# Order of the first layer's input: chunk 0's norm and one value block ahead of chunk 1

## The chip, the cores and the metric

The kernel runs on one core of one Trainium2 chip. The metric is the device time of one execution in microseconds (us). Shown is the median of several runs; a profiled execution of its own gives the trace. TensorE (PE), VectorE (DVE), ScalarE (ACT) and GpSimd (POOL) each work through a queue of their own in order; all DMAs are issued from SyncE's queue (SP).

## The reference

A trunk of two layers over 1040 tokens (16 learned ones ahead of 1024), width 1024, everything in float32. Each layer normalizes its input, projects it with one wide matrix, runs two kinds of attention (a differential one and one with a forget gate), gates the result and projects it back:

```python
h = jnp.concatenate([meta, x], axis=1)
for l in range(DEPTH):                       # DEPTH = 2
    hn = rmsnorm(h, norm_gain[l])            # h * rsqrt(mean(h*h) + eps) * gain
    proj = hn @ w_in[l]                      # queries, keys, values, gates
    ...                                      # two attentions, gated: do, fo
    h = h + jnp.concatenate([do, fo], axis=-1) @ w_out[l]
out = rmsnorm(h, final_gain)
```

The change concerns the very first steps: the norm of `x` in layer 0, and the first values computed from it.

## The kernel before

**Tiling.** The tokens lie in three chunks of 336, 384 and 320 columns (0, 1, 2), each of three blocks of at most 128 tokens, nine blocks in all. The activations are kept transposed, width on the partitions, in KT = 8 slices of 128. Every float32 product is made of three passes with a high and a low part of each operand: `acth`, `actl` for the normalized input, `whi`, `wlo` for a weight.

**The start.** A string START holds the order in which the start is emitted; a letter is a step and the digit after it a chunk:

- `x2`: loads chunk 2's rows of `x` (`first_load`, L346); chunks 0 and 1 are loaded ahead of the string.
- `S`: sums of squares of the chunk's rows (two on ACT, L362, one on DVE, L358) and their reciprocal root in a dozen DVE operations on tiny tiles (L364, L201 to L207).
- `T`: 24 transposes on PE (L183), three to a slice, each slice copied out of PSUM by ACT (L380) and stored to DRAM.
- `N`: PE spreads the root over all partitions (six matmuls, L179 `pj<-ident,rsy`), ACT copies that (`gs`, L392), and then eight pieces follow (`norm_piece`, L401 to L404): DVE multiplies into a buffer `tc` of which there are three, ACT makes the high part, and DVE (even slices) or POOL (odd slices) the low part.
- `v`: a half of one block's value projection, 12 of 24 matmuls `pj<-acth` against the weights of `v_unit`. With the second half the block is split into a high and a low part by ACT (L426) and DVE (L428). So `v v` is a block, and chunk 0 has three of them. The projections take turns in two PSUM buffers `pj`, which `N` uses as well.

After the string come the constants (`load_constants`, among them eight small loads of the lambdas), the last three value blocks (`drive(v0)`), and then the layer proper, which begins with the keys' unit k0.

**What sets the order.** PE's order is the program's, by hand (`manual_schedule`): a PE instruction that waits holds up all that is emitted behind it. The other engines' queues and SP's are sorted by a planner from a modelled course of the program, an operation emitted earlier going first where both are ready. Once written, they too are worked through in order. Below, "block 0" to "block 8" are the value blocks, T0 to N2 the steps of START.

Of the kernel before, what the change touches and what calls it, by code (L numbers as in the profile page):

```python
# [45 lines left out]
ORDER = ("k0 q0 k1 q1 | g0 k2 v1 q2 | g1 k3 q3 | g2 v2 k4 q4 | g3 k5 q5 | g4 v3 h k6 q6 | k7 q7 g5 | "  # L46
         "g6 g7")

START = "T0 S0 N0 x2 S1 T1 N1 v v v v v v S2 T2 N2 v v v v v v"


COL, TRAN, TURN = 0.458e-3, 0.109, 0.088
# [32 lines left out]
def trunk_kernel(ctx, tc, x, meta, norm_gain, w_in, fbias, lq1, lk1, lq2, lk2,  # L85
# [1028 lines left out]
    with tc.manual_schedule(engines={mybir.EngineType.PE}):  # L1114
# [7 lines left out]
        hs, rs = [None] * 3, [None] * 3  # L1122
        for op in START.split():
            c = int(op[1:] or 0)
# [75 lines left out]
```

## Time and profile before

| what | us |
|---|---|
| median of 3 runs | 1605.58 (1605.05 to 1609.21) |
| profiled execution | 1607.66 |
| its span in the trace | 1605.6 |
| PE busy in the span | 1487.7 |
| first matmul of k0 | 68.24 |

The profile's times count from the span's start. A timeline row holds start, length, engine, line, operation, output and inputs, and how many instructions are merged in it; brackets give the engine's idle time just before and what ended it. PE's matmuls overlap, so the distance between two starts is the pace, not the length of one.

### The profile page before, as it was taken

The numbers are of one execution on the slowest core, as the hardware profiler recorded it, in microseconds if no ns is written. First come the engines' busy times: TensorE is split into PE (matmuls) and PEld (weight loads), VectorE is DVE, ScalarE is ACT, GpSimd is POOL, SyncE is SP. The second block draws the span as 40 slices with busy tenths as digits, with TensorE's granted clock in tenths as the row PEclk, the third lists the DMA queues.
The fourth block names the chain that finished last, engine by engine and source line by source line (L and its number), as shares of the span: only waits on it lengthen the run. The fifth ranks groups of instructions, "written<-read, shape, count | busy, mean of one in ns | idle before, by whom it ended". The sixth has DMA issues, their size and how long they took to land. (4 is left out here: it accounts for less than half of the span.)

```text
span 1605.6 us, 30162 instructions
## 1 busy us (share of the span) xinstructions
PE 1487.7 (93%) x9932; PEld 1420.1 (88%) x9932; DVE 1043.0 (65%) x3024; ACT 828.6 (52%) x2067; POOL 689.6 (43%) x1125
## 2 busy tenths in 40 slices
PE   5988999999999999988998999899999999888997
PEld 4888989999999999887988899799999999886897
DVE  6488747866755575757655976586756555547564
ACT  6455545545654565543334654465556556446443
POOL 3353233404442445456846341442253344344674
PEclk9999999999999999998999999999999999999999
DMA  9252212223321324555434231332242222335454
GB/s 242 64 113 73 71 51 75 72 36 86 69 66 42 79 67 126 170 151 159 147 70 106 69 87 33 88 81 50 43 93 59 52 69 61 87 96 159 138 158 139
DMA packets 181725, 148.28 MB, mean 92 GB/s; under 512 B 19624, under 2 KB 177120, under 8 KB 181568
## 3 DMA queue, kind: packets, MB, share of 16 engines
q1 hardware_dynamic: 181568, 146.34, 34.6%
q8 instruction: 79, 1.29, 0.3%
q14 instruction: 78, 0.64, 0.1%
HBM read 117.70 MB, written 28.59 MB: 91 GB/s over the span
## 5 line engine op out<-in xcount | busy, mean ns | idle before, releaser
L179 PE MATMUL pj<-acth,whi 128*128 128x320 f32 (+2 forms) x1536 | 517.0, 337 | 22.9 <-ACT tc L416 7.6
L179 PE MATMUL pj<-acth,wlo 128*128 128x320 f32 (+2 forms) x1536 | 498.1, 324 | 2.7 <-POOL wlo L263 2.7
L179 PE MATMUL pj<-actl,whi 128*128 128x320 f32 (+2 forms) x1536 | 497.8, 324 | 0.0
L263 POOL TENSOR_TENSOR wlo<-wst,whi 128x256 fp32r<-128x256 f32 (+1 forms) x320 | 249.3, 788 | 244.0 <-ACT whi L259 216.3
L179 PEld LDWEIGHTS pj<-acth,whi 128*128 128x128 f32 x1536 | 295.9, 193 | 28.0 <-ACT tc L416 8.2
L179 PEld LDWEIGHTS pj<-acth,wlo 128*128 128x128 f32 x1536 | 295.2, 192 | 3.8 <-POOL wlo L263 3.2
L179 PEld LDWEIGHTS pj<-actl,whi 128*128 128x128 f32 x1536 | 293.9, 191 | 0.0
L660 ACT ACTIVATE e<-e,mn 80x80 f32<-80x80 f32 (+8 forms) x288 | 225.2, 782 | 124.2 <-DVE mn L652 121.6
L744 DVE TENSOR_TENSOR atl<-tp,ath 128x320 fp32r<-128x320 f32 (+8 forms) x432 | 191.5, 450 | 97.7 <-ACT ath L743 92.9
L743 ACT ACTIVATE ath<-tp 128x320 fp32r<-128x320 f32 (+8 forms) x432 | 167.6, 403 | 138.2 <-PE tp L183 131.1
L179 PE MATMUL sc<-kt,qq 128*128 128x296 f32 (+9 forms) x480 | 178.8, 375 | 25.2 <-DVE mn L652 17.3
L259 ACT ACTIVATE whi<-wst 128x256 fp32r<-128x256 f32 (+1 forms) x304 | 124.1, 415 | 150.4 <-DMA wst<-in_w_out_dram 50.7
L693 POOL TENSOR_SCALAR e<-e,rl 80x80 f32<-80x80 f32 (+2 forms) x144 | 110.8, 770 | 165.6 <-DVE rl L692 160.2
L183 PE MATMUL tp<-ident,e 128*128 128x128 f32 (+2 forms) x1080 | 180.7, 275 | 0.9 <-POOL e L693 0.8
L179 PE MATMUL po<-ath,v 128*128 128x256 f32 (+5 forms) x576 | 167.1, 331 | 13.2 <-ACT ath L743 9.9
L179 PE MATMUL pj<-whi,acth 128*128 128x256 f32 (+3 forms) x576 | 166.4, 289 | 6.7 <-DVE v L428 5.8
L179 PE MATMUL pj<-wlo,acth 128*128 128x256 f32 (+3 forms) x576 | 164.2, 285 | 2.1 <-POOL wlo L263 1.4
L179 PE MATMUL pj<-whi,actl 128*128 128x256 f32 (+3 forms) x576 | 163.8, 284 | 0.6 <-POOL actl L404 0.6
L179 PE MATMUL sc<-kt,ql 128*128 128x296 f32 (+9 forms) x480 | 159.7, 335 | 0.0
L179 PE MATMUL po<-atl,v 128*128 128x256 f32 (+5 forms) x432 | 136.8, 317 | 12.8 <-DVE atl L744 11.7
L183 PEld LDWEIGHTS tp<-ident,e 128*128 128x128 f32 (+2 forms) x1080 | 137.1, 140 | 7.0 <-POOL e L693 2.3
L179 PEld LDWEIGHTS sc<-kt,qq 128*128 128x128 f32 (+1 forms) x480 | 91.5, 191 | 37.7 <-DVE mn L652 23.8
(166 smaller groups left out, 2471.5 us busy)
## 6 DMA issues: line engine op xcount, KB each, us to landing
wst<-in_w_in_dram SPq DMA_DIRECT2D x256, 128.0 KB
wst<-in_w_out_dram SPq DMA_DIRECT2D x192, 128.0 KB
cb<-cscr SPq DMA_DIRECT2D x16, 520.0 KB
cb<-in_rope_dram SPq DMA_DIRECT2D x20, 320.0 KB
cb<-in_rope_dram SPq DMA_DIRECT2D x16, 384.0 KB
oscr<-ta SPq DMA_DIRECT2D x22, 192.0 KB
oscr<-ta SPq DMA_DIRECT2D x26, 160.0 KB
cb<-in_rope_dram SPq DMA_DIRECT2D x12, 336.0 KB
```

Source lines behind the costliest of these rows:

```text
L179: nc.tensor.matmul(o, a, b, start=start, stop=stop)
L183: nc.tensor.transpose(o, a, idn)
L259: nc.scalar.activation(hi, sg_, AF.Copy)
L263: eng.tensor_tensor(lo, sg_, hi.bitcast(F32), ALU.subtract)
L660: nc.scalar.activation(e[rows, :ext], e[rows, :ext], AF.Exp, scale=-1.0, bias=mn[rows, len(pcs) - 1:len(pcs)], accum_out=l[rows, :])
L693: nc.gpsimd.tensor_scalar(e[rows, :ext], e[rows, :ext], r[rows, 0:1], 1.0, ALU.mult, ALU.mult)
L743: nc.scalar.activation(ah[:kz, n0:w], tp[:kz, n0:w], AF.Copy)
L744: nc.vector.tensor_tensor(al[:kz, n0:w], tp[:kz, n0:w], ah[:kz, n0:w].bitcast(F32), ALU.subtract)
```

## The change

START alone is changed. Before, T0 S0 N0, the loads of chunk 2, then S1 T1 N1 and all three blocks of chunk 0 (six `v`), then chunk 2's steps. After, S0 T0 N0, the loads, then block 0 (`v v`), then T1 S1 N1, then blocks 1 and 2, and T2 ahead of S2. No operation is added or removed.

```diff
-START = "T0 S0 N0 x2 S1 T1 N1 v v v v v v S2 T2 N2 v v v v v v"
+START = "S0 T0 N0 x2 v v T1 S1 N1 v v v v T2 S2 N2 v v v v v v"
```

## Rows read from the trace of the kernel before

**Rows 1.** PE's waits, 0 to 112 us: engine, line, releaser: total, times, longest

```profile
PE pj L179 <- DVE v L428: 4.8, 3, 2.4
```

**Rows 2.** Timeline of PE, 17 to 69 us: start, length, instructions

```profile
17.52 2.21 PE L183 MATMUL sc<-ident,e 128*128 128x128 f32 x9
...
23.64 1.54 PE L183 MATMUL sc<-ident,e 128*128 128x128 f32 x6 [0.58 <-ACT hc L380]
26.81 1.65 PE L179 MATMUL pj<-ident,rsy 128*128 128x128 f32 x6 [1.63 <-DVE rsv L236]
...
32.40 0.35 PE L179 MATMUL pj<-whi,actl 128*80 128x256 f32 x1 [0.39 <-POOL actl L404]
32.59 0.28 PE L179 MATMUL pj<-whi,acth 128*128 128x256 f32 x1
...
37.82 0.35 PE L179 MATMUL pj<-whi,acth 128*128 128x256 f32 x1 [2.23 <-DVE v L428]
...
40.73 4.58 PE L183 MATMUL sc<-ident,e 128*128 128x128 f32 x24
...
46.25 0.39 PE L179 MATMUL pj<-whi,acth 128*128 128x256 f32 x1
...
60.97 0.55 PE L179 MATMUL pj<-whi,acth 128*128 128x256 f32 x1 [2.37 <-DVE v L428]
...
68.24 0.31 PE L179 MATMUL pj<-acth,whi 128*128 128x336 f32 x1
```

**Rows 3.** Windows of 10 us: length; busy of PE, PEld, DVE, ACT, POOL; clock, DMA

```profile
20.00:30.00 10.00, 6.38 (x30) 5.27 (x31) 8.98 (x22) 8.52 (x21) 3.97 (x5) 0.67 1.07 272
30.00:40.00 10.00, 7.38 (x59) 6.96 (x59) 9.96 (x25) 5.27 (x14) 5.14 (x6) 0.99 0.94 251
```

**Rows 4.** Timeline of ACT, 14 to 26 us

```profile
14.09 1.06 ACT L362 ACTIVATE kt<-e 128x1024 f32<-128x1024 f32 x1 [1.89 <-DMA e<-in_x_dram]
...
15.14 1.11 ACT L380 ACTIVATE qq<-sc 128x336 f32<-128x336 f32 x3
...
17.29 1.06 ACT L362 ACTIVATE kt<-e 128x1024 f32<-128x1024 f32 x1 [1.04 <-DMA e<-in_x_dram]
...
18.98 0.44 ACT L392 ACTIVATE gs<-pj 128x336 f32<-128x336 f32 x1
...
23.10 1.25 ACT L380 ACTIVATE hc<-sc 128x384 f32<-128x384 f32 x3
```

**Rows 5.** Timeline of DVE, 19 to 61 us

```profile
19.82 1.99 DVE L401 SCALAR_TENSOR_TENSOR tc<-qq,ng,gs 128x336 f32<-128x336 f32 x3
...
21.81 0.74 DVE L263 TENSOR_TENSOR wlo<-wst,whi 128x256 fp32r<-128x256 f32 x2
...
28.23 1.38 DVE L358 CUSTOM_DVE_ANT_0 kt<-e 128x1024 f32<-128x1024 f32 x1 [0.98 <-DMA e<-in_x_dram]
...
46.91 1.48 DVE L401 SCALAR_TENSOR_TENSOR tc<-qq,ng,gs 128x320 f32<-128x320 f32 x3 [3.86 <-ACT gs L392]
...
60.39 0.23 DVE L146 CUSTOM_DVE_ANT_0 tc<-tc 128x64 f32<-128x64 f32 x1 [2.64 <-DMA tc<-in_lambda_k_dram]
```

**Rows 6.** Timeline of POOL: the last low part of N0, of N1, of N2

```profile
31.24 1.11 POOL L404 TENSOR_TENSOR actl<-tc,acth 128x336 fp32r<-128x336 f32 x1 [2.71 <-ACT acth L402]
...
39.36 3.06 POOL L404 TENSOR_TENSOR actl<-tc,acth 128x384 fp32r<-128x384 f32 x2
...
54.74 0.87 POOL L404 TENSOR_TENSOR actl<-tc,acth 128x320 fp32r<-128x320 f32 x1 [0.93 <-ACT acth L402]
```

**Rows 7.** Windows of 1 us, columns as in rows 3; the clock is third from the end

```profile
23.00:24.00 1.00, 0.42 (x3) 0.36 (x3) 1.00 (x3) 1.00 (x4) 0.82 (x1) 0.71 0.84 338
...
30.00:31.00 1.00, 1.00 (x9) 1.00 (x9) 0.96 (x4) 0.78 (x3) 0.00 (x0) 0.87 1.03 43
...
44.00:45.00 1.00, 1.00 (x6) 0.57 (x6) 0.00 (x0) 0.73 (x3) 0.00 (x0) 1.00 0.74 271
...
64.00:65.00 1.00, 1.00 (x9) 1.00 (x9) 0.00 (x0) 0.00 (x0) 0.00 (x0) 0.81 0.00 0
```

## The prediction

> **What bounds the kernel now.** PE is busy nearly throughout, so I read the stretch in which the change lies as a chain on PE: what holds up the first matmul of k0, at 68.24 us [rows 2]? From there on PE's order is the same in both versions, and k0's weights can only take the buffers that block 8 gives back, so all that follows shifts with that start. The change is worth what it moves k0's start, and no more, unless the other engines' queues come out differently sorted.
>
> I read three things in the order in which they lie. First the timeline of PE: T1 begins at 17.52 and is stretched by waits for ACT; N1's spreading begins at 26.81; block 0 follows and ends with a wait for POOL's last low part of chunk 0; block 1 starts at 32.59, block 2 only at 37.82 after an idle 2.23 us, T2 at 40.73, block 3 at 46.25 [rows 2]. So block 0 is ready to run long before its input is: T1 and N1 fill a time in which PE would wait for N0 anyway. Second, PE's waits: those for the splitting of value blocks (DVE v L428) are 4.8 us, nearly all of it in two places, at 37.82 and at 60.97 [rows 1, 2]. Third, what holds N0: it begins on DVE at 19.82 and ends on POOL at 31.24 + 1.11 = 32.35 [rows 5, 6]. In that time DVE is busy for 8.98 of the first 10 us and 9.96 of the next, ACT for 8.52 and 5.27 [rows 3]: DVE is the tighter of the two, and it carries pieces of chunk 1 and chunk 2 as well as N0.
>
> **The change, part by part.** Nothing is added or taken away; two things move on PE's queue.
>
> *Block 0 ahead of T1: what it costs.* T1 and the spreading of N1 now lie behind block 0, that is behind the end of N0, and no longer in its shadow. T2 with N2's spreading, the same steps at full clock, took 46.25 - 40.73 = 5.52 us [rows 2], and blocks 1 and 2 follow at 40.73 - 37.82 = 2.91 us each [rows 2]. From T1's new start to T2's start that is 5.52 + 2 x 2.91 = 11.34 us.
>
> *The clock.* Block 0 drips through behind N0, so PE is little used ahead of T1, as it is in the kernel before between 17.5 and 26.8, where the granted clock fell from 2.4 to 1.2 GHz within the slice 23 to 24 (mean 0.71) [rows 7]. It came back in the slice 30 to 31 (0.87), some 3.45 us after PE began to run without a break at 26.81, and again 3.4 us after the start at 60.97 (slice 64 to 65, 0.81) [rows 2, 7]. At the lower clock six transposes took 1.54 us, 0.257 each, against 4.58/24 = 0.191 at the higher [rows 2]. If T1 begins at the lower clock and gets the higher one after 3.45 us, it loses 3.45 x (1 - 0.191/0.257) = 0.9 us. Sum 12.24 us.
>
> *What it saves.* The same stretch of the kernel before, from block 1's start to T2's start, is 40.73 - 32.59 = 8.14 us, and it holds the idle time before block 2: (37.82 - 32.59) - 2.91 = 2.32 us [rows 2]. That was block 0's splitting, which DVE did late between N1's pieces, with only two `pj` buffers. After the change T1 stands between block 0 and the next use of its buffer, and T2 between block 2 and block 3; this cover hides the splitting. If it didn't, the 2.32 us would come back.
>
> So the change breaks even if T1 starts at 40.73 - 12.24 = 28.5 us, and each us by which N0 ends sooner or later than that counts in full.
>
> *When does N0 end now?* Without T1's copies (three took 1.25 us on ACT at 23.10 [rows 4]) it resembles N2, whose eight pieces also ran with no transposes beside them: 46.91 to 54.74 + 0.87 = 55.61, 8.70 us [rows 5, 6]; at 336 columns instead of 320, 9.1 us. From 19.82 that is 28.95. On DVE two low parts of weights (0.74 us [rows 5]) come between, and chunk 1's root, for which N2 had the splitting of value blocks instead; I add 0.74 and let the rest cancel, and a last 0.24 from the end of N0 to the next step on PE (32.35 to 32.59). T1 starts at 29.9, **1.4 us late**. The bounds: with no filler 29.2, a loss of 0.7; with N0 as slow as before, 32.59, a loss of 4.1. I take the value near the lower end because N2 is the nearest row, in form and in its neighbours.
>
> *N1 and N2 behind it.* N1 lasted from about 31 to 39.36 + 3.06 = 42.42 [rows 6], some 11.4 us, with much else on DVE; now its first piece can start 6.5 to 7 us after T1's start, near 37, and it ends near 47 to 48. Block 3 starts near 47.6 and needs the last slice at its end, near 50: covered by 2 us. N2 follows block 3's start as before.
>
> *S0 ahead of T0, T2 ahead of S2, SP.* They work on different engines, except for ACT; S0's squares went ahead of T0's copies before, by their readiness, so I cost this at nothing. Of T1's steps the store of chunk 1 moves later on SP, by some 6 us; its readers come late in the layer, so nothing. The rope tables behind it on SP are for k0 at 68. The store leaves the saturated DMA stretch (DMA share 1.07 [rows 3]) and can't make the weights later. The `x2` loads stay where they are.
>
> Sum: +0.7 (bounds) to +4.1, taken **+1.4 us** on k0's start and on the end. The profiled execution took 1607.66 with a span of 1605.6; the median of the runs is 1605.58, 2.1 below. The difference goes on the median: 1605.6 + 1.4 = 1607.0.
>
> **Rivals.**
>
> *Slower, N0 gains nothing.* In the kernel before, DVE's queue holds chunk 2's sum of squares inside N0: it waited 0.98 us for its load and took 1.38 [rows 5], before N0's last pieces. N2 had no such guest. If the planner leaves it there, T1 starts 2.36 us later, at 32.3: 1607.0 + 2.4 = 1609.4. It decides from the point at which the queue has that operation ahead of N0's last piece. For it: loads and their order don't change. Against: N0 goes faster in the planner's course too, and has precedence.
>
> *Slower, the clock stays down through T1.* Then T1 takes 24 x 0.257 = 6.2 us instead of 4.52 + 0.9, and N1's spreading and block 1 pay for the 3.4 us at half the rate, 1.7 us: together +2.5, 1609.5; with the rival above 1611.9. Against it: in T2, transposes alone, the clock was still 1.00 in the slice 44 to 45, more than 3 us after its start [rows 7]. For it: T1 before the change is the only stretch that goes from the higher to the lower clock with transposes running. The Trainium skill, "TensorE: Matmul & The Clock Gate", section "Part 4: PE-mode transpose", says that transposes don't count as PE activity in the way matmuls do and that full clock doesn't engage for them; by it the time would be 1609.5. The slice in T2 shows at least that they did not let the clock fall here; that they can raise it, no row shows.
>
> *Faster, N0 starts sooner.* ACT's queue had two of chunk 1's squares ahead of N0's needs: at 14.09 after 1.89 us of waiting for the load, so that T0's copies went on only at 15.14, and at 17.29 after 1.04, ahead of `gs` at 18.98 [rows 4]. S1 now stands behind T1 in the string; sorted behind T0 and `gs`, N0 would start up to 1.89 + 1.06 + 1.04 + 1.06 = 5.1 us sooner. But block 0 needs the weights' last low parts (21.81 + 0.74), so I count 4: 1603.0. Against: S1 stood behind N0 already and went first, because its load was modelled early.
>
> *Faster, the stall at 60.97 goes.* Block 7 waited 2.37 us because DVE's queue held a lambda product at 60.39 that waited 2.64 us for its load [rows 2, 5], and lost 1.7 us more by the clock. Another sorting would give up to 4.1: 1602.9, and with the rival above 1598.9. Nothing in the change speaks for it: N2 and the lambdas keep their places.
>
> *Not only what it says.* The planner sorts the queues of the whole program anew. If that isn't undone by k0, waits of 2 to 2.4 us such as these two appear or go anywhere: 2.4 either way, 1604.6 to 1609.4.
>
> **How the numbers follow.** Chances: forecast (1605.6 to 1608.5) 0.42; N0 gains nothing 0.16; the clock stays down, alone or with that, 0.12; N0 starts sooner 0.12; the stall goes, alone or with that, 0.08; sorting elsewhere 0.10. A measurement of this kernel can tell about 0.3%, 4.8 us, from no change. Beyond it lie on the slower side the clock together with a slow N0 and a part of the sortings, 0.14; on the faster side the two gains together and a part of the sortings, 0.10; within, 0.76. The range goes from the single gains (1602.9) to the two losses together (1611.9), with a little more on the faster side for both gains in part: 1602.0 to 1612.0.
>
> **What would show it.** In the changed kernel's PE timeline: T1's start (29.9 forecast, 28.5 breaks even, 32.3 the slow N0), no idle time of 2 us between blocks 1 and 2, T2 12.2 us after T1's start, k0 near 69.7, and the same stall near block 7. The granted clock in T1's second half tells the clock rival. I would be wrong if N0 starts well before 19, if block 3 waits for N1, or if k0's shift and the end's shift differ by over 2 us.

## The result, and the profile after

| | before | after |
|---|---|---|
| median of 6 runs, us | 1607.41 (1605.05 to 1609.30) | 1616.95 (1612.60 to 1618.27) |
| profiled execution, us | 1607.66 | 1612.60 |
| its span, us | 1605.6 | 1610.8 |
| T1 starts | 17.52 | 28.43 |
| N1's spreading starts | 26.81 | 38.00 |
| T2 starts | 40.73 | 46.32 |
| k0 starts | 68.24 | 76.03 |

The change is slower: after takes 1.0055 times as long as before, 95% interval 1.0038 to 1.0073, or 8.8 us more (6.1 to 11.7). The forecast was 1607.0 in a range from 1602.0 to 1612.0. Of the 10.0 us between forecast and measurement 1.8 lie in before itself, whose median stands at 1607.41 with six runs instead of 1605.58 with three; the rest is what the change cost beyond the forecast's 1.4. Nearly the whole loss can be seen on PE's queue ahead of k0. This is PE's timeline of the changed kernel, with the columns of [rows 2]:

```profile
19.73 0.50 PE L179 MATMUL pj<-whi,acth 128*80 128x256 f32 x1 [4.73 <-ACT acth L402]
...
28.43 4.53 PE L183 MATMUL sc<-ident,e 128*128 128x128 f32 x24
...
38.00 1.65 PE L179 MATMUL pj<-ident,rsy 128*128 128x128 f32 x6 [5.03 <-DVE rsv L236]
...
46.32 1.72 PE L183 MATMUL sc<-ident,e 128*128 128x128 f32 x9
...
49.50 2.92 PE L183 MATMUL sc<-ident,e 128*128 128x128 f32 x15 [1.46 <-ACT qq L380]
...
54.12 0.58 PE L179 MATMUL pj<-whi,acth 128*128 128x256 f32 x1
...
70.30 0.36 PE L179 MATMUL pj<-whi,acth 128*128 128x256 f32 x1 [2.03 <-DVE v L428]
...
76.03 0.31 PE L179 MATMUL pj<-acth,whi 128*128 128x336 f32 x1
```

Block 0 now runs from 19.73 with N0 and ends at 28.43, where T1 begins. T1 takes 4.53 us, and then PE stands still for 5.03 us: it waits for a DVE tile of the root of chunk 1, which N1's spreading reads. In the kernel before that wait was 1.63 us and lay in a time in which PE had nothing else to run [rows 2].

Why is the root so late? ACT's timeline of the changed kernel gives the answer:

```profile
29.47 3.31 ACT L380 ACTIVATE hc<-sc 128x384 f32<-128x384 f32 x6
32.68 0.48 ACT L380 ACTIVATE hcb<-sc 128x384 f32<-128x384 f32 x1
33.05 1.06 ACT L362 ACTIVATE kt<-e 128x1024 f32<-128x1024 f32 x1
34.09 1.05 ACT L362 ACTIVATE kt<-e 128x1024 f32<-128x1024 f32 x1
35.13 0.49 ACT L380 ACTIVATE hcb<-sc 128x384 f32<-128x384 f32 x1
```

The two sums of squares of chunk 1 (L362) stand in ACT's queue behind seven of T1's eight copies, at 33.05 and 34.09. Before, they ran at 14.09 and 17.29, as their loads landed [rows 4]. The third square of the chunk is DVE's, and the rest of the root follows there. DVE's timeline of the changed kernel:

```profile
29.81 1.21 DVE L358 CUSTOM_DVE_ANT_0 kt<-e 128x1024 f32<-128x1024 f32 x1
...
35.38 0.17 DVE L364 TENSOR_SCALAR rsv<-rsv 128x3 f32<-128x3 f32 x1
...
37.79 0.15 DVE L207 SCALAR_TENSOR_TENSOR rsy<-rst,rsy 128x3 f32<-128x3 f32 x1
```

From the end of the second square (34.09 + 1.05 = 35.14) to the last operation of the root (37.79 + 0.15 = 37.94) the chain takes 2.8 us, and 0.06 later the spreading starts.

**Where k0's 7.79 us come from** (76.03 - 68.24):

- T1's start, against the break-even of 28.5: -0.07.
- T1 to T2: 46.32 - 28.43 = 17.89, where the working counted 12.24: +5.65. The wait is 5.03 of it. T1 took 4.53, 0.9 less than the 5.42 that were counted for it with the clock's loss, but then the clock fell during the wait, and N1's spreading with blocks 1 and 2 took 46.32 - 38.00 = 8.32 instead of 6.82, 1.5 more.
- T2 to block 3: 54.12 - 46.32 = 7.80 instead of 5.52: +2.28. T2 waits 1.46 for ACT's copies, which stand in ACT's queue behind N1's last piece (48.60), and N2's spreading took 1.77 (54.12 - 52.35) instead of 1.00 before (46.25 - 45.25), at the lower clock.
- Block 3 to k0: 76.03 - 54.12 = 21.91 instead of 68.24 - 46.25 = 21.99: -0.08. That the two agree is chance. In before the lower clock followed the stall near block 7 (0.50 in the slice 62 to 64); in after it lies in block 3 instead, and the clock stays up behind the stall.

The sum is 7.78. The granted clock in the stretch, in windows of 2 us of the changed kernel (columns as in [rows 3]):

```profile
30.00:32.00 2.00, 2.00 (x12) 2.00 (x11) 1.03 (x2) 1.56 (x4) 0.00 (x0) 0.53 1.05 79
32.00:34.00 2.00, 0.97 (x9) 0.66 (x7) 0.00 (x0) 2.00 (x5) 0.00 (x0) 1.00 0.95 262
34.00:36.00 2.00, 0.00 (x0) 0.00 (x0) 1.67 (x6) 2.00 (x6) 0.00 (x0) 0.83 1.06 399
...
40.00:42.00 2.00, 2.00 (x11) 2.00 (x10) 1.71 (x6) 1.23 (x3) 0.00 (x0) 0.50 0.00 0
...
54.00:56.00 2.00, 2.00 (x10) 1.88 (x11) 1.23 (x3) 1.08 (x3) 0.00 (x0) 0.50 0.15 49
...
72.00:74.00 2.00, 2.00 (x19) 2.00 (x18) 0.98 (x6) 0.89 (x4) 0.00 (x0) 1.00 0.00 0
```

PE stood still from 32.96 to 38.00; the clock fell from 2.4 to 1.2 GHz within the slice 34 to 36 and was still there in 40 to 42.

**Behind k0.** The next long wait of PE, 3.77 us for a DVE tile `mn`, stands in both kernels; it ends at 95.96 in before and at 103.74 in after, that is 7.78 later, the shift of k0. The span is only 5.2 us longer in the profiled executions, so 2.6 us came back later. The clock gave part of it. First before, then after, in windows of 2 us behind the end of that wait:

```profile
96.00:98.00 2.00, 2.00 (x8) 2.00 (x9) 1.94 (x8) 1.52 (x7) 1.84 (x4) 0.50 0.98 80
98.00:100.00 2.00, 2.00 (x9) 2.00 (x9) 1.60 (x8) 0.99 (x4) 1.36 (x2) 0.50 1.00 82
100.00:102.00 2.00, 2.00 (x9) 2.00 (x8) 2.00 (x11) 1.75 (x6) 0.55 (x1) 0.52 1.05 70
```

```profile
104.00:106.00 2.00, 2.00 (x8) 2.00 (x9) 1.97 (x9) 1.39 (x8) 1.92 (x3) 0.50 1.00 68
106.00:108.00 2.00, 2.00 (x12) 2.00 (x12) 1.60 (x8) 1.12 (x5) 1.14 (x2) 0.75 1.00 82
```

In before PE worked at the lower clock from the end of the wait, 95.96, to 102 (0.50, 0.50, 0.52: 6.0 us), in after from 103.74 to 107 (0.50, and 0.75, which is half of a slice: 3.3 us). Work at half the rate loses half of the time at the lower clock, 3.0 against 1.6 us, so 1.4 of the 2.6 us lie there by this estimate. This execution is also the quickest of the six of after; over all runs the difference is 8.8 us with an interval that holds the 7.8.

### The profile page after: what moved, and what is told of

Same layout as the page of the kernel before. It is cut to its first block, busy times and chain, and to the rows that moved or that the text cites. A ratio compares the mean times of both kernels' runs of the same rounds, so it can differ in the third digit from the quotient of the medians.

```text
span 1610.8 us, 30160 instructions
## 1 busy us (share of the span) xinstructions
PE 1493.4 (93%) x9932; PEld 1424.2 (88%) x9932; DVE 1039.7 (65%) x3024; ACT 828.6 (51%) x2067; POOL 686.7 (43%) x1125
## 3 DMA queue, kind: packets, MB, share of 16 engines
q1 hardware_dynamic: 181568, 146.34, 34.5%
```

## The experiments

**The theories.** A string step can be late for more than one reason, so two theories stood against each other. Theory A: the loss comes from S1's place behind T1 in the string. T1 takes a buffer for `hcb` from the pool `kt` (`hc_tiles`, tag `kt`), and S1's squares are written to `junk = big("kt", 4)`, a tile from the same pool that nobody reads. The planner hands out the buffers of a tag in the program's order, so a square of chunk 1 can't be placed until T1's first copy into `hcb`, the seventh of eight, is. That would be an order in the queues and no wait for a buffer at run time: the third square, on DVE, wrote to a `kt` tile at 29.81, ahead of that copy at 32.68. Theory B: the loss comes from block 0's place. Ahead of T1 it puts chunk 1's chain behind the end of N0, whoever is first of S1 and T1.

The other swaps in the string need no runs: with S0 and T0 alone in the new order, every engine's queue is that of the kernel before, instruction for instruction; and with T2 and S2 back in the old order, the queues are those of the first experiment.

**S1 ahead of T1, block 0 in its new place**

```diff
-START = "S0 T0 N0 x2 v v T1 S1 N1 v v v v T2 S2 N2 v v v v v v"
+START = "S0 T0 N0 x2 v v S1 T1 N1 v v v v T2 S2 N2 v v v v v v"
```

> Block 0 stays ahead of T1, but S1 goes ahead of T1 in the string (S0 T0 N0 x2, block 0, S1 T1 N1, blocks 1 and 2, then as after). Theory A, chunk 1's sums of squares come too late because S1 stands behind T1: the idle time of 5.03 us ahead of N1's spreading is under 1 us, T1 starts near 29.9, k0 between 68 and 71 us, the time 0 to 0.2% above the kernel before. Theory B, block 0 ahead of T1 on PE is itself the cost: k0 at 74 us or later, the time 0.4 to 0.6% above the kernel before, as after the change.

Measured: 1610.41 us, 1.0027 times before (1.0015 to 1.0040). PE's timeline:

```profile
30.71 1.15 PE L183 MATMUL sc<-ident,e 128*128 128x128 f32 x9
...
34.13 0.83 PE L179 MATMUL pj<-ident,rsy 128*128 128x128 f32 x6
...
46.98 1.41 PE L179 MATMUL pj<-ident,rsy 128*128 128x128 f32 x6 [1.92 <-DVE rsv L236]
...
70.55 0.32 PE L179 MATMUL pj<-acth,whi 128*128 128x336 f32 x1
```

N1's spreading follows T1 without a wait, and T2 starts at 40.48, a little sooner than before the change. The time is above what theory A expected, because a wait of the same kind has moved on: N2 now waits 1.92 us for the root of chunk 2. ACT's timeline of the same kernel has chunk 2's squares right behind the first copy into `hcb`, and the root's small operations on DVE then come among N1's pieces, up to 46.93:

```profile
34.02 0.49 ACT L380 ACTIVATE hcb<-sc 128x384 f32<-128x384 f32 x1
34.40 1.05 ACT L362 ACTIVATE kt<-e 128x1024 f32<-128x1024 f32 x1
```

So with S1 ahead of T1 about half of the loss in time is gone, and 5.5 of the 7.79 us on k0. The run doesn't yet tell the pool from the place.

**The new string with block 0 in its old place**

```diff
-START = "S0 T0 N0 x2 v v T1 S1 N1 v v v v T2 S2 N2 v v v v v v"
+START = "S0 T0 N0 x2 T1 S1 N1 v v v v v v T2 S2 N2 v v v v v v"
```

> Block 0 stays where it was before (behind T1 and N1), and only S and T are swapped, T1 ahead of S1 and T2 ahead of S2. Theory A: chunk 1's squares go on ACT behind T1's first copy into the buffer hcb, N1's spreading starts at 31 to 33 us instead of 26.81, k0 2 to 5 us later than before, the time 0.1 to 0.3% above. Theory B: the time is that of the kernel before within 0.1%, k0 at 68 to 69.

Measured: 1615.57 us, 1.0044 (1.0028 to 1.0061). PE's timeline, then ACT's:

```profile
34.59 1.65 PE L179 MATMUL pj<-ident,rsy 128*128 128x128 f32 x6 [11.03 <-DVE rsv L236]
...
76.07 0.31 PE L179 MATMUL pj<-acth,whi 128*128 128x336 f32 x1
```

```profile
23.23 0.51 ACT L380 ACTIVATE hcb<-sc 128x384 f32<-128x384 f32 x1
23.59 1.09 ACT L362 ACTIVATE kt<-e 128x1024 f32<-128x1024 f32 x1
24.63 1.09 ACT L362 ACTIVATE kt<-e 128x1024 f32<-128x1024 f32 x1
```

The squares stand right behind the first copy into `hcb` here too, and k0 starts at 76.07, as late as in the change, although block 0 was not moved at all. The loss was larger than expected: the squares are done by 25.7, but the root's small operations stand on DVE behind chunk 2's sum of squares (28.65) and among N0's last pieces, to 34.5, so that PE stood still for 11.03 us. S1 behind T1 costs as much as the whole change on k0, with block 0 in its old place.

**The new string as it is, the unread tile from another pool**

```diff
-            junk = big("kt", 4)
+            junk = big("cb", 2)
```

> The changed kernel with its own string, but the buffer into which the squares are written (nobody reads it) comes from the pool tag cb instead of kt, so that it no longer stands in line behind T1's hcb for a kt buffer. Theory A in its narrow form, the shared buffer tag is what holds S1 behind T1's copies: the squares of chunk 1 run on ACT before T1's copies, no wait over 1 us ahead of N1's spreading, k0 at 68 to 71 us, the time 0 to 0.2% above the kernel before. Theory A in its wide form, the order in the string alone holds S1 back: squares still behind T1's copies, k0 near 76, the time 0.5% above. Theory B: k0 at 74 or later, the time 0.4 to 0.6% above, wherever the squares stand.

Measured: 1607.59 us, 1.0013 (1.0002 to 1.0025). ACT's timeline, then PE's:

```profile
13.23 1.06 ACT L362 ACTIVATE cb<-e 128x1024 f32<-128x1024 f32 x1 [1.82 <-DMA e<-in_x_dram]
...
16.59 1.06 ACT L362 ACTIVATE cb<-e 128x1024 f32<-128x1024 f32 x1 [1.19 <-DMA e<-in_x_dram]
```

```profile
31.74 4.24 PE L183 MATMUL sc<-ident,e 128*128 128x128 f32 x24
35.82 0.83 PE L179 MATMUL pj<-ident,rsy 128*128 128x128 f32 x6
...
68.90 0.32 PE L179 MATMUL pj<-acth,whi 128*128 128x336 f32 x1
```

With the string of the change untouched, the squares of chunk 1 are back at 13.23 and 16.59, N1 doesn't wait, and k0 starts 0.66 us later than before instead of 7.79. The ratio falls from 1.0055 to 1.0013. That shows theory A in its narrow form: it is the shared pool tag that made S1's place in the string matter. Theory B falls for the main part; what the rest of the change costs with the squares early, block 0's place in it, is 0.13% (0.02 to 0.25), 2.1 us (0.3 to 4.0).

**Can N0 be made to end sooner?** What is left of the change's price is N0's end: T1 starts at 31.74 here, but at 28.43 in the change, where no square of chunk 1 lay in N0's way. Three runs hold chunk 1's squares on ACT behind `gs`, on top of the other pool: one with the new string, one with the string of before (to tell block 0's place apart), one that holds chunk 2's squares as well. The edits add lines, so L404 and L406 in their views are L402 and L404 of the kernel before.

```diff
-        nc.scalar.activation(rb[:, :w], pt[:, :w], AF.Copy)
+        spread[c] = nc.scalar.activation(rb[:, :w], pt[:, :w], AF.Copy).ins
...
-                rs[c] = first_scale(c, xs[c])
+                with tc.issue_after(spread[0]) if c == 1 else ExitStack():
+                    rs[c] = first_scale(c, xs[c])
```

The new string:

> The changed kernel with the squares' buffer from cb, and chunk 1's two squares on ACT queued behind N0's gs. Theory A (both squares and N0 want ACT early; neither may go far ahead of the other): gs at 15 us, N0's first piece near 16.5 instead of 19.8, squares done by 19, no wait over 1 us ahead of N1's spreading, T1 starts at 28 to 30, k0 at 66 to 68, the time 0 to 0.15% below the kernel before. Theory B, block 0 ahead of T1 costs as such: T1 no earlier than 31, k0 at 69 or later, the time 0.1 to 0.3% above.

Measured: 1608.36 us, 1.0006 (0.9991 to 1.0022), T1 at 31.81. N0 did not end sooner, so the expected gain is a miss. ACT's timeline, then PE's, of this kernel:

```profile
19.03 1.04 ACT L362 ACTIVATE cb<-e 128x1024 f32<-128x1024 f32 x1
...
20.68 1.21 ACT L404 ACTIVATE acth<-tc 128x336 fp32r<-128x336 f32 x3
...
28.77 1.06 ACT L362 ACTIVATE cb<-e 64x1024 f32<-64x1024 f32 x1 [1.89 <-DMA e<-in_x_dram]
```

```profile
21.20 0.50 PE L179 MATMUL pj<-whi,acth 128*80 128x256 f32 x1 [6.08 <-ACT acth L404]
...
29.04 0.50 PE L179 MATMUL pj<-whi,actl 128*80 128x256 f32 x1 [2.14 <-DVE actl L406]
...
31.81 4.05 PE L183 MATMUL sc<-ident,e 128*128 128x128 f32 x24
...
70.42 0.32 PE L179 MATMUL pj<-acth,whi 128*128 128x336 f32 x1
```

The hold keeps the squares behind `gs`, but both of them (the first at 15.51, the second at 19.03) still lie ahead of N0's first high part at 20.68, and a square of chunk 2 at 28.77, which first waited 1.89 us for its load, is in N0's last pieces.

The string of before, with the same two edits:

> The kernel before, block 0 in its old place, with the same two edits (squares' buffer from cb, chunk 1's squares on ACT behind gs). Theory A: N0 starts near 16.5 here too and ends 1 to 3 us sooner; k0 at 65.5 to 67.5, the time 0.05 to 0.2% below the kernel before, and block 0's place alone (this run against the one with block 0 ahead) is worth less than 0.1%. Theory B: this run is 0.2% or more below the one with block 0 ahead.

Measured: 1610.43 us, 1.0019 (1.0004 to 1.0034). PE's timeline:

```profile
32.97 1.65 PE L179 MATMUL pj<-ident,rsy 128*128 128x128 f32 x6 [7.77 <-DVE rsv L236]
...
73.76 0.32 PE L179 MATMUL pj<-acth,whi 128*128 128x336 f32 x1
```

Held like this, chunk 1's second square fell behind two of T1's copies (20.24 on ACT), the root's small operations came on DVE among N0's pieces and behind a square of chunk 2 (28.73), and PE waited 7.77 us for the root. In the order of before the root of chunk 1 is needed early, and what makes it late here costs at once. Both theories' expectations missed, and the run doesn't tell block 0's place apart, since it has a wait for the root that the run with the new string lacks.

The new string with chunk 2's squares held behind N0's last piece too (the same form of edit, on ACT and DVE):

> As the run with S1 held behind gs and block 0 ahead, and chunk 2's squares held behind N0's last piece on ACT and on DVE. Theory A: no wait of PE within block 0 for a square of chunk 2, T1 starts 1 to 2 us sooner than in the run without this hold (27 to 29), k0 0.5 to 2 us sooner, the time 0.05 to 0.2% below the kernel before. Theory B: no gain on k0.

Measured: 1607.74 us, 1.0011 (0.9997 to 1.0025). PE's timeline:

```profile
29.63 2.12 PE L183 MATMUL sc<-ident,e 128*128 128x128 f32 x9
...
35.30 0.96 PE L179 MATMUL pj<-ident,rsy 128*128 128x128 f32 x6
...
72.30 0.32 PE L179 MATMUL pj<-acth,whi 128*128 128x336 f32 x1
```

T1 starts 2.2 us sooner than in the first of the three runs, about as expected, but k0 comes 1.9 us later than there in this execution (72.30 against 70.42), a miss, and the time is the same within the intervals. The clock took the gain: it was granted at 0.50 in every slice of 1 us from 29 to 35, N1's spreading followed T1's start by 35.30 - 29.63 = 5.67 us, against 3.89 in the first of the three (35.70 - 31.81), and from 46 to 52 it was at 0.50 again. The four versions in which the squares don't wait for `hcb` lie between 1.0006 and 1.0019 with intervals that overlap; the runs don't rank them, and none beats the kernel before.

## Why the prediction was wrong

The sum missed a term. Point by point:

**What was right.** PE's order ahead of k0 did bound the change: the 7.79 us that k0 lost are what the next long wait lost too (7.78). T1's start, 28.43, was within 1.5 us of the forecast 29.9, and on the break-even of 28.5, but only with chunk 1's squares out of N0's way, the re-sorting that made the root late; in the third experiment it was 31.74. The idle time between blocks 1 and 2 is gone, block 3 did not wait for N1, and the stall near block 7 stayed (2.03 us at 70.30, against 2.37 [rows 2]). So the string's visible effect, block 0 against T1, was worth about nothing, as the sum had it; where the squares are not held, k0 moves by +0.66 for a forecast of +1.4, and the time by 2.1 us (0.3 to 4.0). That this came so near is partly luck: there T1 started 3.24 us behind the break-even, and 10.42 us from T1 to T2 (42.16) instead of 12.24, and 20.74 from block 3 (48.16) to k0 instead of 21.99, made up for it.

**The step that failed: S1 behind T1.** The working moved S1 past T1 in the string, and weighed this only as a gain for N0, in the rival that N0 starts sooner. That it could make chunk 1's root late was never priced, and the 12.24 us from T1 to T2 hold no wait for it: the working's paragraph on the swapped steps costs S0 and T0, T2 and S2 at nothing and leaves S1 and T1 out. The squares had run at 14.09 and 17.29 before, and the working took it that readiness alone would keep them there. The code had the reason against it in sight: L358 and L362 write their squares to a `kt` tile, and T1's `hcb` is a `kt` tile. Priced from the rows it would have been large. If the squares stand behind T1's seventh copy, the root follows them by two squares and its DVE chain, and N1 waits for all of this. After shows 5.03 us of waiting for it and, with the clock and T2's wait behind, 7.8 us in all.

**The clock term.** It was about right in size, but stood on a wrong pace. The sum took T2's 4.52 us as what 24 transposes need at the higher clock. In the first experiment T1 ran at a granted clock of 1.00 (30 to 40): its first nine transposes took 1.15 us, and N1's spreading followed its start by 34.13 - 30.71 = 3.42 us, a wait of 0.38 for ACT included. In the last experiment, at 0.50, nine took 2.12 and the spreading followed after 5.67. So T2 did not run at PE's own pace; ACT's copies of it, five in 2.72 us at 42.50, came about as slowly as its transposes, three to a copy, and which of the two held the other isn't shown. T1 of the change, at 0.50 to 0.53 up to 32, took 4.53 us, 1.1 more than 3.42, for a forecast loss of 0.9; with the base of 4.52 the 5.42 us were 0.9 too many. That hid a part of what came behind the wait: the spreading took 1.65 us, against 0.83 in the first and third experiments, where PE had not stood still, and with blocks 1 and 2 the loss at the lower clock was 1.5 us, which the sum did not have.

**The rivals.** *N0 gains nothing* fell: N0's first piece began at 16.49 instead of 19.82 [rows 5], and its last low part ended at 28.08 instead of 32.35 [rows 6]. *N0 starts sooner* thus came true in its cause, S1's squares behind T0's copies and `gs` (15.03 instead of 18.98 [rows 4]), but not in its size. N0 began 3.33 us sooner on DVE and ended 4.27 sooner than before, 1.6 sooner than the 29.7 of the forecast (28.95 + 0.74). It didn't gain the 4 us over the forecast that the rival counted, since ACT's queue then waited for weights. ACT's timeline of the changed kernel:

```profile
15.03 0.45 ACT L392 ACTIVATE gs<-pj 128x336 f32<-128x336 f32 x1 [0.79 <-PE pj L179]
...
17.76 0.42 ACT L259 ACTIVATE whi<-wst 128x256 fp32r<-128x256 f32 x1 [2.28 <-DMA wst<-in_w_in_dram]
...
18.89 0.42 ACT L259 ACTIVATE whi<-wst 128x256 fp32r<-128x256 f32 x1 [0.71 <-DMA wst<-in_w_in_dram]
19.21 0.47 ACT L402 ACTIVATE acth<-tc 128x336 fp32r<-128x336 f32 x1
```

The first high part of N0 stands behind conversions of weights that wait 2.28 and 0.71 us for their loads. The same re-sorting that gave N0 its start took the 5.03 us from N1, and the prediction counted only the first. Without the hold, in the third experiment, *N0 gains nothing* nearly came true: chunk 2's sum of squares stands at 28.16 on DVE, in N0 as before, and T1 starts at 31.74, near this rival's 32.3. *The clock stays down through T1* fell in the changed kernel, where it rose about 3.5 us into T1, as the sum had it; in the last experiment it came true. *The stall goes* fell: 2.03 us of it stayed, and only the time at the lower clock behind it went. *Sorting elsewhere* has little: behind the start, the engines' queues are the same but for a few dozen instructions near the end of the last layer, and no run parts these from the rest.

**The signs that were named.** N0 started at 16.49, "well before 19", so the first sign came true, and it was the trace of what went wrong: the squares had left N0's way. Block 3 did not wait for N1. That k0's shift and the end's shift differ by over 2 us came true in the profiled execution, where they differ by 2.6, and not against the difference over all runs (7.8 and 8.8). A difference of this size between two single executions says little here: the clock alone gave some 1.4 of it.

**Open.** Which of the four versions without the hold by `hcb` is quickest, and why k0's shift in one execution and the ratio over runs differ by 1 to 3 us (e.g. 4.1 us of k0 against 0.11%, 1.8 us, in the last run), is not settled; single executions differ in where the clock falls.

## What to carry to other kernels

When a step moves past another in a program that a planner sorts, list the buffers that both take, by pool tag, as carefully as the data: a tile that nobody reads can hold a step behind another if it shares a tag with it, and here a change of tag alone took most of the loss back. Price every moved step in both directions; an order that lets one chain start sooner because another went later has to be charged with what waits for the other. And of work that ran long before it was needed, ask what kept it early, before taking it for granted that it stays there.

## What the runs showed of the hardware

Transposes alone brought TensorE's clock back in the changed kernel. T1, 24 transposes and nothing else from 28.43, ran at a granted clock of 0.53 (1.2 GHz nearly throughout) in the slice 30 to 32 and at 1.00 (2.4 GHz) in 32 to 34; ahead of it PE had run block 0 with breaks, at 0.50. They needn't do so within one T1: in the last experiment T1 began at 29.63, paused for 0.30 us ahead of 32.05, and the clock was still at 0.50 in the slice 34 to 35; the slice 35 to 36, into which N1's spreading falls, has 0.72. The Trainium skill, "TensorE: Matmul & The Clock Gate", section "Part 4: PE-mode transpose", says that full clock doesn't engage for transposes; the trace of the changed kernel differs, and the measurement decides.

After one and the same wait of 3.77 us the clock stayed at the lower level for 6.0 us in one execution (before) and for 3.3 us in the other (after), with the same instructions behind it. In single executions that is worth a microsecond or two at each long wait, as much as the smaller terms of the sum.
